# Attention steps 7 to 15 with scores ahead of the value product and row maxima ahead of its output's halves; four top-k instructions moved from steps 5 and 6 to step 3

## Chip, cores and metric

The kernel runs on one core of one Trainium2 chip. The metric is the device time of one execution in microseconds (us); lower is better.

## What is computed

One decoder block on 512 tokens of width 1024: a combined input projection, a gated mixer (A), a sparse attention (B), a gated merge, a feed-forward part and a final norm, all in float32. The change lies in mixer B. Cut to what matters:

```python
def block(i):                                   # 128 queries, i = 0..3
    score = sum_h wib[h] * relu(qib[h] @ ki.T)  # the indexer
    score = where(causal, score, -inf)
    sel_score, sel_idx = lax.top_k(score, 128)  # 128 keys of each query
    att = q @ k[sel_idx].T * 128 ** -0.5        # 8 heads, 2 key heads
    p = softmax(where(isfinite(sel_score), att, NEG_INF))
    return p @ v[sel_idx]
```

The kernel doesn't gather. It turns the scores of the indexer into a mask over all keys (0 for a chosen one, -1e30 else) by 16 rounds of "find the 8 largest, overwrite them", and adds the mask to the full scores before the softmax.

## The kernel before

The tile scheduler is switched off: every engine executes its instructions in the order in which the Python code issues them, and waits at an instruction until what it needs is there. So the order of the calls in the code is the order of each engine's queue.

A float32 product is made of three TensorE matmuls on rounded halves (`mm3`, L107 to L109: high by high, low by high, high by low). So every operand is first split: ScalarE (ACT in the profile) copies the high half, VectorE (DVE) subtracts it from the source to give the low half.

**Units and steps.** Attention runs over 16 units u, in `aun`: query block i = 3, 2, 1, 0 (512, 384, 256, 128 keys) by four pairs of heads. `at_step(s)` runs for s = 0 to 18, each step a slice of a pipeline over units. Steps and units are counted from 0 here. NT = 4: units 0 to 3 have their probabilities transposed by VectorE and a trip through DRAM, units 4 to 15 by TensorE. NU = 16. The pieces, with the letters used below:

- qk(u), `at_qk`: scores of unit u, six matmuls into PSUM banks 2 and 3 (two for the last four units).
- soft_a(u), `at_soft_a`: on VectorE, two instructions (L1394) that read qk(u) and the mask `sco`, and give masked scores and row maxima; then a scaling of the maxima (L1396). Until it has read them, banks 2 and 3 are taken.
- exp(u), `at_exp`, on ScalarE (L1404). inv(u), `at_inv`: reciprocal of the sums on VectorE (L1409) and one head's scaling on ScalarE (L1411); soft_b(u): the other head's scaling on VectorE (L1420). From unit 9 on soft_b does both, with the reciprocal (L1418).
- T(u), `at_T`: transposes on TensorE (pT, L1461), then th(u) on ScalarE (L1466) and tl(u) on VectorE (L1467), their high and low halves. For units 0 to 3: turn(u) on VectorE (tn, L1425), out(u) to DRAM by SyncE's queue (L1432), ld(u) back by GpSimd's queue (POOL, L1438), and halves th(u), tl(u) by `at_halves` (L1448, L1449).
- pv(u), `at_pv`: the value product, 3 matmuls for each 128 keys, into PSUM bank 0 (bank 1 for units 0 to 3). yb(u), `at_yb`: its output's halves, high on ScalarE (L1489), low on VectorE (L1490).
- `gb_part(n)`: matmuls of another projection, pgb, six for each of its 32 parts, that fill TensorE between the attention's pieces. `GBN` says how many parts each step takes: none in step 8, one in step 7, two in steps 9 to 15.

A step s from 7 on issues inv(s-1), pv(s-3), yb(s-3), qk(s), soft_a(s), T(s-2), soft_b(s-1), the split of a later query, exp(s), and then pgb; steps 5 to 8 also carry pv(s-5) and yb(s-5).

**Top-k** of blocks 2 and 1 isn't finished when attention starts. Its instructions lie in a list `bg` in order; `run_bg(us)` takes as many from it as the given budget pays by a cost written beside each. `need_sco(i)` in `at_soft_a` empties the list up to block i's mask if it isn't complete when it is needed. The dictionary in `at_step` sets the budget of each step.

Weights come by SyncE's queue into three buffers `raw`, and are split into `hi` (L164) and `lo` (L168), 128 by 1024 at a time; L263 is a weighted row sum on VectorE for later stages.

Of the kernel before, what the change touches and what calls it, by code (L numbers as in the profile page):

```python
# [58 lines left out]
def block_kernel(ctx: ExitStack, tc: tile.TileContext, x, x_t, w_in,  # L59
# [36 lines left out]
    def bank(k, name="bank"):  # L96
        return (two[0] if k > 5 else psum).tile([128, 512], F32, name=name, tag=f"b{k}", bufs=1)

    def f(ap):
        return ap.bitcast(F32)  # L100
# [4 lines left out]
    def mm3(o, wl, rl, start, stop, **kw):  # L105
        (wh, wlo), (rh, rlo) = wl, rl
        T.matmul(o, wh, rh, start=start, stop=False, **kw)  # L107
        T.matmul(o, wh, rlo, start=False, stop=False, **kw)  # L108
        T.matmul(o, wlo, rh, start=False, stop=stop, **kw)  # L109
# [357 lines left out]
    def t512(name, dt=F32):  # L467
        return base.tile([128, 512], dt, name=name, tag="t512", bufs=3)
# [444 lines left out]
    def run_bg(us):  # L913
        owed[0] += us
        while bg and owed[0] > 0:
            cost, fn = bg.popleft()
            fn()
            owed[0] -= cost

    def need_sco(i):  # L920
        while len(bg) > left.get(i, 99):
            bg.popleft()[1]()
# [402 lines left out]
    def at_split(u, apart=False):  # L1325
        i, hp = aun[u]
        if i == 0:
            return lambda: None
        qh = mid.tile([128, 2, 128], F32R, name="qh", tag="qh", bufs=2)
        ql = mid.tile([128, 2, 128], F32R, name="ql", tag="ql", bufs=2)  # L1330
        AS["q", u] = (qh, ql)
        src = qf[hp][:, :, i * 128:(i + 1) * 128]
        A.activation(qh, src, AF.Copy)
        if apart:
            return lambda: V.tensor_sub(ql, src, f(qh))
        V.tensor_sub(ql, src, f(qh))
# [25 lines left out]
    NU = len(aun)  # L1362
    gbp, gbt, gbn = {}, {}, [0]
    S2B, yb = [], []
    NT = 4
    pd = [dram.tile([32, 4096], F32, name=f"pd{k}") for k in range(NT)]

    def at_qk(u):
        i, hp = aun[u]
        nn = (i + 1) * 128  # L1370
        g = hp // 2
        for e in range(2):
            p = bank((4 if u < NT and u % 2 else 2) + e, "qk")
            AS["s", u, e] = p
            if i == 0:
                T.matmul(p[:, :nn], qf[hp][:, e, :nn], k_pl[:, g], start=True, stop=True)
                continue
            qh, ql = AS["q", u]
            mm3(p[:, :nn], (qh[:, e], ql[:, e]), (kk[0][:, g, :nn], kk[1][:, g, :nn]), True, True)

    def at_soft_a(u):
        i, hp = aun[u]
        need_sco(i)
        n = (i + 1) * 128
        k = u % 2 if u < NT else (u - NT + 2) % 3
        if k == 2:
            pt = [t512("pt"), t512("pt")]
        else:
            t = mid.tile([128, 2, S], F32, name="pt", tag=f"A{k}", bufs=1)
            pt = [t[:, 0], t[:, 1]]  # L1390
            AS["w", u] = t
        mx = tiny.tile([128, 8], F32, name="mx", tag="mx", bufs=3)
        for e in range(2):
            V.tensor_tensor_reduce(out=pt[e][:, :n], in0=AS["s", u, e][:, :n], in1=sco[i], scale=1.0,  # L1394
                                   scalar=-3.4e38, op0=OP.add, op1=OP.max, accum_out=mx[:, e:e + 1])
        V.tensor_scalar(mx[:, 2:4], mx[:, 0:2], -SCALE, None, op0=OP.mult)  # L1396
        AS["p", u] = (pt, mx)
# [9 lines left out]
    def at_inv(u):  # L1407
        pt, mx = AS["p", u]
        V.reciprocal(mx[:, 6:8], mx[:, 4:6])  # L1409
        n = (aun[u][0] + 1) * 128  # L1410
        A.mul(pt[1][:, :n], pt[1][:, :n], mx[:, 7:8])  # L1411

    def at_soft_b(u):
        i, hp = aun[u]
        n = (i + 1) * 128
        pt, mx = AS["p", u]
        if u >= NT + 5:
            V.reciprocal(mx[:, 6:8], mx[:, 4:6])  # L1418
        for e in range(1 if u < NT + 5 else 2):
            V.tensor_scalar(pt[e][:, :n], pt[e][:, :n], mx[:, 6 + e:7 + e], None, op0=OP.mult)  # L1420

    def at_turn(u):
        t = AS["t", u] = (mid if u < 3 else base).tile([128, 4, 4, 2, 32], F32, name="tn", tag=("G2", "G3", "G2", "gate")[u],
                                                       bufs=1)
        V.transpose(t.rearrange("p c k e j -> p e k c j"),  # L1425
                    AS["w", u].rearrange("p e (k c j) -> p e k c j", c=4, j=32))

    def at_out(u):
        t = AS["t", u].rearrange("p c k e j -> p (c k) (e j)")
        to = pd[u].rearrange("a (m r x) -> r a m x", r=4, x=64)  # L1430
        for r in range(4):
            SY.dma_start(to[r], t[32 * r:32 * r + 32])  # L1432

    def at_in(u):
        t = AS["l", u] = (mid if u % 2 else vmid).tile([128, 1024], F32, name="ld", tag="G1" if u % 2 else "L", bufs=1)
        rows = pd[u].rearrange("a (c m) -> c a m", c=4)
        for c in range(4):
            P.dma_start(t[32 * c:32 * c + 32], rows[c])  # L1438
# [12 lines left out]
    def at_T(u):  # L1451
        i, hp = aun[u]
        pt, _ = AS["p", u]
        th, tl = AS["t", u] = th_tl("A2", "A3")
        ev = []
        for s0 in range(0, i + 1, 2):
            ns = min(2, i + 1 - s0)
            p = bank(4 + s0 // 2, "pT")
            for s in range(ns):
                for e in range(2):  # L1460
                    T.transpose(p[:, (s * 2 + e) * 128:(s * 2 + e + 1) * 128],  # L1461
                                pt[e][:, (s0 + s) * 128:(s0 + s + 1) * 128], ident)
            o, ol = (x[:, s0:s0 + ns].rearrange("p s n -> p (s n)") for x in (th, tl))
            ev.append((o, ol, p[:, :ns * 256]))
        for o, ol, p in ev:
            A.activation(o, p, AF.Copy)  # L1466
            V.tensor_sub(ol, p, f(o))  # L1467

    def at_pv(u):
        i, hp = aun[u]  # L1470
        th, tl = AS["t", u]
        g = hp // 2
        p = bank(1 if u < NT else 0, "pv")
        for s in range(i + 1):
            mm3(p[:, :256], (v_hi[:, s, g * 128:(g + 1) * 128], v_lo[:, s, g * 128:(g + 1) * 128]),
                (th[:, s], tl[:, s]), s == 0, s == i)
        AS["o", u] = p[:, :256]

    def at_yb(u):
        i, hp = aun[u]  # L1480
        o = slice(i * 128, (i + 1) * 128)
        yh, yl = S2B[hp][:, :, o], S2B[4 + hp][:, :, o]
        p = AS["o", u]
        if u < NT:
            yh, yl = (x.rearrange("p e (r j) -> p e r j", r=4) for x in (yh, yl))
            p = p.rearrange("p (r e j) -> p e r j", r=4, e=2)
        else:
            p = p.rearrange("p (e n) -> p e n", e=2)
        A.activation(yh, p, AF.Copy)  # L1489
        V.tensor_sub(yl, p, f(yh))  # L1490
# [30 lines left out]
    def at_step(s):  # L1521
        if 1 <= s <= NT + 5:
            at_inv(s - 1)
        if s == 0:
            at_qk(0)
            at_split(2)
        pvs = [u for u in (s - 5, s - 3) if 0 <= u < NU and (u < NT) == (u == s - 5)]
        for u in pvs[-1:] if s >= NT + 3 else []:
            at_pv(u)
            at_yb(u)  # L1530
        q = s + 1 if s + 1 < NT else s if s >= NT else NU
        if q < NU:
            at_qk(q)
        if s < NU:
            at_soft_a(s)
        if s == 2:
            pa_last[0]()
        if NT <= s - 2 < NU:
            at_T(s - 2)
        if 0 < s <= NU:  # L1540
            at_soft_b(s - 1)
        if 2 <= s < NT + 2:
            at_in(s - 2)
        if 1 <= s < NT + 1:
            at_turn(s - 1)
            at_out(s - 1)
        n = s + 3 if s + 1 < NT else s + 2
        low = at_split(n, True) if n < NU and s != NT - 1 else lambda: None
        if s < NU:
            at_exp(s)  # L1550
        low()
        run_bg({0: 2.0, 1: 0.5, 5: 0.5, 6: 1.8, 7: 1.8}.get(s, 0))
        if s == NT:
            at_halves(0)
        if s - 5 in range(NT):
            gb_part(GBN[s] // 2)
            at_pv(s - 5)
            at_yb(s - 5)
        gb_part(GBN[s] - (GBN[s] // 2 if s - 5 in range(NT) else 0))
        if s - 4 in range(1, NT):  # L1560
            at_halves(s - 4)
        if s >= NT + 4:
            gb_evac()
# [3 lines left out]
    def pa_tasks():  # L1567
        au_tasks()
        at_step(pa_step[0])
        pa_step[0] += 1  # L1570
# [18 lines left out]
    for s in range(2, NU + 3):  # L1589
        at_step(s)  # L1590
# [500 lines left out]
    for q in range(-2, NQ):  # L2091
        g, u = 2 + q // 2, q % 2
# [299 lines left out]
```

## Time and profile before

| what | value |
|---|---|
| median of 3 runs (lowest, highest) | 783.99 us (782.96, 785.48) |
| the profiled execution's own time | 783.45 us |
| its span | 781.7 us |
| granted TensorE clock in it | 0.996 |
| busy share of the span: TensorE, VectorE, ScalarE, GpSimd | 98%, 87%, 60%, 24% |
| steps 2 to 18 of the attention in the span | about 290 to 369 us |
| TensorE's waits for other engines in the trace after 370 us | none shown |

In rows of the timeline the columns are start, duration, engine, line, operation, output and inputs, shape, how many were merged, and in brackets the idle time of the engine ahead of it with what released it. A window's row gives for each engine its busy time and how many instructions lie in it, then the granted clock (1.00 is full), the share of the DMA engines and GB/s. A TensorE matmul's end is modelled: how fast matmuls run is read from start to start. A row of the waits tells who waited for whom, the sum, how often and the longest.

### The profile page before, as it was taken

The page shows a single profiled execution, that of the slowest core. Times are in us where ns is not written, and L with a number is a line of the kernel's source. Part 1 is how long each engine was busy: PE and PEld are TensorE (multiplying, and loading weights), DVE is VectorE, ACT ScalarE, POOL GpSimd, SP SyncE. Part 2 cuts the span into 40 slices and gives each one's busy share as a digit, 9 for nine tenths or more (in the row PEclk, how much of TensorE's full clock was granted, in tenths as well). Part 3 has the DMA queues.
Part 4 walks back from the last instruction along what each step waited for, and adds up shares of the span by engine and source line. Part 5 has one row for each costly group of instructions (what it writes and reads, how often), then busy time and mean ns, then how long its engine had stood idle before and what let it go on. Part 6 is the DMA issues. An engine that isn't in the chain of part 4 may idle for free.

```text
span 781.7 us, 13086 instructions
## 1 busy us (share of the span) xinstructions
PE 767.6 (98%) x4867; PEld 695.9 (89%) x4867; DVE 677.0 (87%) x1108; ACT 469.4 (60%) x831; POOL 185.9 (24%) x270
## 2 busy tenths in 40 slices
PE   8999999999999999899999999999999999999996
PEld 6899899999888888788888899999999999888885
DVE  8879768888899998887797879989999888998886
ACT  6665568577443347666446677555666666666654
POOL 4882322320164503100010000322121322100002
PEclk9999999999999999999999999999999999999999
DMA  9957676986779739539592503979797967656762
GB/s 344 415 193 175 160 195 185 260 216 197 212 239 267 219 91 230 137 93 377 196 277 48 195 2 108 254 236 309 247 283 211 275 197 200 176 182 207 219 223 111
DMA packets 58978, 163.43 MB, mean 209 GB/s; under 512 B 17121, under 2 KB 17761, under 8 KB 58914
## 3 DMA queue, kind: packets, MB, share of 16 engines
q1 hardware_dynamic: 44240, 118.63, 44.7%
q0 software_dynamic: 14096, 43.01, 24.4%
q10 hardware_dynamic: 578, 0.95, 0.3%
q8 instruction: 38, 0.62, 0.3%
q14 instruction: 26, 0.21, 0.1%
HBM read 152.06 MB, written 33.30 MB: 237 GB/s over the span
## 4 chain that ended last, share of the span: by engine, by line
PE 84%; DVE 9%; DMA 2%; ACT 2%; issue 2%; POOL 1%; SPq 0%; POOLq 0%; DVEq 0%; ACTq 0%
PE R L107 8%; PE R L108 8%; PE R L109 8%; PE pb L109 5%; PE pb L108 5%; PE pb L107 5%; PE pfo L109 4%; PE pfo L108 4%; PE pfo L107 4%; PE pav L107 3%; PE pav L108 3%; PE pav L109 3%; PE po L109 2%; PE po L107 2%; PE po L108 2%; DVE sco L901 2%
## 5 line engine op out<-in xcount | busy, mean ns | idle before, releaser
L164 ACT ACTIVATE hi<-raw 128x1024 fp32r<-128x1024 f32 (+4 forms) x90 | 90.3, 1007 | 73.3 <-PE pfo L109 21.8
L168 DVE TENSOR_TENSOR lo<-raw,hi 128x1024 fp32r<-128x1024 f32 (+3 forms) x70 | 81.7, 1168 | 19.8 <-ACT hi L164 18.9
L108 PE MATMUL pfo<-lo,za 128*128 128x512 f32 (+1 forms) x144 | 55.2, 383 | 0.0
L109 PE MATMUL pfo<-hi,za 128*128 128x512 f32 (+1 forms) x144 | 55.2, 383 | 0.0
L107 PE MATMUL pfo<-hi,za 128*128 128x512 f32 (+1 forms) x144 | 55.2, 383 | 0.0
L107 PE MATMUL pb<-h,hi 128*128 128x512 f32 (+1 forms) x128 | 48.5, 379 | 0.0
L109 PE MATMUL pb<-h,lo 128*128 128x512 f32 (+1 forms) x128 | 48.1, 376 | 0.0
L108 PE MATMUL pb<-h,hi 128*128 128x512 f32 (+1 forms) x128 | 48.1, 376 | 0.0
L426 POOL COPY sm<-sm 128x1 f32<-128x1 f32 x36 | 25.6, 710 | 82.4 <-ACT sm L425 82.4
L108 PE MATMUL R<-tb,hi 128*128 128x256 f32 x160 | 44.2, 276 | 0.0
L107 PE MATMUL R<-tb,sx 128*128 128x256 f32 x160 | 44.2, 276 | 0.0
L108 PE MATMUL R<-tb,sx 128*128 128x256 f32 x160 | 44.2, 276 | 0.0
L109 PE MATMUL R<-tb,sx 128*128 128x256 f32 x160 | 44.2, 276 | 0.0
L107 PE MATMUL R<-tb,hi 128*128 128x256 f32 x160 | 44.2, 276 | 0.0
L109 PE MATMUL R<-tb,lo 128*128 128x256 f32 x160 | 44.2, 276 | 0.0
L168 POOL TENSOR_TENSOR lo<-raw,hi 128x1024 fp32r<-128x1024 f32 x12 | 30.6, 2548 | 31.0 <-ACT hi L164 31.0
L406 POOL DMA_DIRECT2D wsum<-in_w_ffn_out_dram x24 | 19.6, 838 | 73.3 <-DMA wsum<-wsum 42.9
L107 PEld LDWEIGHTS pfo<-hi,za 128*128 128x128 f32 x144 | 27.1, 188 | 5.4
L108 PEld LDWEIGHTS pfo<-lo,za 128*128 128x128 f32 x144 | 27.1, 188 | 5.3
L109 PEld LDWEIGHTS pfo<-hi,za 128*128 128x128 f32 x144 | 27.1, 188 | 5.2
L263 DVE CUSTOM_DVE_ANT_0 mraw<-mraw,csb,cols 128x1024 f32<-128x1024 f32 x20 | 28.4, 1426 | 2.0 <-DMA mraw<-in_w_shsc_dram 2.0
L108 PEld LDWEIGHTS R<-tb,hi 128*128 128x128 f32 x160 | 30.0, 188 | 0.0
(443 smaller groups left out, 2883.7 us busy)
## 6 DMA issues: line engine op xcount, KB each, us to landing
raw<-in_w_ffn_in_dram SPq DMA_DIRECT2D x44, 512.0 KB, 6.1
raw<-in_w_in_dram SPq DMA_DIRECT2D x36, 512.0 KB, 4.8
wsum<-in_w_ffn_out_dram POOLq DMA_DIRECT2D x30, 512.0 KB, 8.0
mraw<-in_w_shsc_dram SPq DMA_DIRECT2D x28, 512.0 KB, 4.7
raw<-wsum SPq DMA_DIRECT2D x20, 512.0 KB, 3.6
s<-in_w_shsc_dram SPq DMA_DIRECT2D x14, 512.0 KB, 8.0
raw<-in_w_ffn_out_dram SPq DMA_DIRECT2D x13, 512.0 KB, 4.5
wsum<-wsum POOLq DMA_DIRECT2D x10, 512.0 KB, 5.9
```

Of the source, the lines that this page charges most:

```text
L107: T.matmul(o, wh, rh, start=start, stop=False, **kw)
L108: T.matmul(o, wh, rlo, start=False, stop=False, **kw)
L109: T.matmul(o, wlo, rh, start=False, stop=stop, **kw)
L164: A.activation(hi[:, :m], e["raw"][:, :m], AF.Copy)
L168: e["lo"].tensor_sub(lo[:, :m], e["raw"][:, :m], f(hi[:, :m]))
L263: V.tensor_tensor_reduce(out=raw[:, c], in0=raw[:, c], in1=(csb if s > 1 else pc)[:, c], scale=scale, scalar=sums.pop(0), op0=OP.mult, op1 ...
L406: P.dma_start(wsum_at(n, c), src, max_dma_last_dim=4096, accum_op=OP.add)
L426: P.tensor_copy(t, t)
L901: V.match_replace(out=sco[i], in_to_replace=m8s[i], in_values=sco[i], imm_value=TAKEN)
```

## The change

From step 7 to step 15 qk(s) is issued first after inv, ahead of pv(s-3), and soft_a(s) ahead of yb(s-3). The budget of top-k gets an entry for step 3 and a smaller one for step 6.

```diff
     def at_step(s):
         if 1 <= s <= NT + 5:
             at_inv(s - 1)
+        late_q = NT + 3 <= s < NU
+        if late_q:
+            at_qk(s)
         if s == 0:
             at_qk(0)
             at_split(2)
         pvs = [u for u in (s - 5, s - 3) if 0 <= u < NU and (u < NT) == (u == s - 5)]
         for u in pvs[-1:] if s >= NT + 3 else []:
             at_pv(u)
-            at_yb(u)
+            if not late_q:
+                at_yb(u)
         q = s + 1 if s + 1 < NT else s if s >= NT else NU
-        if q < NU:
+        if q < NU and not late_q:
             at_qk(q)
         if s < NU:
             at_soft_a(s)
+        if late_q:
+            at_yb(pvs[-1])
...
-        run_bg({0: 2.0, 1: 0.5, 5: 0.5, 6: 1.8, 7: 1.8}.get(s, 0))
+        run_bg({0: 2.0, 1: 0.5, 3: 1.8, 5: 0.5, 6: 0.9, 7: 1.8}.get(s, 0))
```

VectorE's queue in step 3, as a piece of the difference; tn is turn(2), sco_633 the mask of block 1, and the lo and the reciprocal behind belong to a weight and to step 4:

```order
 L1425 STREAM_TRANSPOSE tn<-pt 128x2x4x4x32
+L898 MAX m_3245<-sco_633 128x8
+L901 MATCH_REPLACE sco_633<-m_3245,sco_633 128x256
+L898 MAX m_3248<-sco_633 128x8
+L901 MATCH_REPLACE sco_633<-m_3248,sco_633 128x256
 L168 TENSOR_TENSOR lo<-raw,hi 128x1024
 L1409 RECIPROCAL mx<-mx 128x2
```

Two rounds of top-k now stand between turn(2) and the weight's low half.

VectorE's queue at the end of step 6 and the start of step 7, before (ql is the low half of a query, yb_3153 belongs to unit 1, yb_3152 to unit 4, the tl of L1449 to unit 2, the reciprocal to unit 6, L1394 to unit 7):

```order
L1335 TENSOR_TENSOR ql<-qf_604,qh 128x256
L901 MATCH_REPLACE sco_633<-m_3377,sco_633 128x256
L898 MAX m_3455<-sco_633 128x8
L901 MATCH_REPLACE sco_633<-m_3455,sco_633 128x256
L904 TENSOR_SCALAR sco_633<-sco_633 128x256
L1490 TENSOR_TENSOR yb_3153<-pv,yb_3149 128x2x128
L1449 TENSOR_TENSOR tl<-ld,th 128x512 x2
L1409 RECIPROCAL mx<-mx 128x2
L1490 TENSOR_TENSOR yb_3152<-pv,yb_3148 128x2x128
L1394 ISA pt,mx<-qk,sco_634 128x384
L1394 ISA mx 128x1
```

And now:

```order
L1335 TENSOR_TENSOR ql<-qf_604,qh 128x256
L1490 TENSOR_TENSOR yb_3153<-pv,yb_3149 128x2x128
L1449 TENSOR_TENSOR tl<-ld,th 128x512 x2
L1409 RECIPROCAL mx<-mx 128x2
L1394 ISA pt,mx<-qk,sco_634 128x384
L1394 ISA mx 128x1
L1394 ISA pt,mx<-qk,sco_634 128x384
L1394 ISA mx 128x1
L1396 TENSOR_SCALAR mx<-mx 128x2
L1490 TENSOR_TENSOR yb_3152<-pv,yb_3148 128x2x128
```

The four top-k instructions of step 6 are gone (its closing one, L904, stands in step 5 in the place of a MAX), and yb(4) has moved from ahead of soft_a(7) to behind it.

TensorE's queue at the start of step 8, as a piece of the difference (qk is unit 8, pv unit 5):

```order
 L108 MATMUL pgb<-h_146,hi 128x512
 L109 MATMUL pgb<-h_144,lo 128x512
+L107 MATMUL qk<-k_hi,qh 128x256
+L108 MATMUL qk<-k_lo,qh 128x256
+L109 MATMUL qk<-k_hi,ql 128x256
+L107 MATMUL qk<-k_hi,qh 128x256
+L108 MATMUL qk<-k_lo,qh 128x256
+L109 MATMUL qk<-k_hi,ql 128x256
 L107 MATMUL pv<-th,v_hi 128x256
 L108 MATMUL pv<-tl,v_hi 128x256
```

The six score matmuls stood behind pv(5)'s nine before and stand ahead of them now; T(6) follows in both. ScalarE's, GpSimd's and SyncE's queues keep their order, and no instruction is added or dropped.

## The prediction

> **What bounds the kernel now.** I read the page first, then the engines' busy time by windows, the waits in the attention stretch, and the timelines of TensorE, VectorE and ScalarE there.
>
> ```profile
> span 781.7 us, 13086 instructions
> ...
> PE 767.6 (98%) x4867; PEld 695.9 (89%) x4867; DVE 677.0 (87%) x1108; ACT 469.4 (60%) x831; POOL 185.9 (24%) x270
> ```
>
> TensorE is the engine that sets the time: a microsecond of it is a microsecond of the span. The windows show where it has holes; its busy time is the number behind the first comma.
>
> ```profile
> 310.00:320.00 10.00, 9.33 (x56) 8.00 (x56) 8.13 (x25) 7.77 (x20) 4.11 (x9) 1.00 1.06 265
> 320.00:330.00 10.00, 8.92 (x63) 7.75 (x61) 7.71 (x23) 6.40 (x17) 0.11 (x1) 1.00 0.32 77
> 330.00:340.00 10.00, 8.56 (x56) 7.78 (x57) 8.82 (x27) 8.07 (x22) 0.00 (x0) 1.00 0.08 13
> 340.00:350.00 10.00, 9.72 (x58) 8.37 (x57) 9.08 (x28) 5.10 (x13) 0.57 (x1) 1.00 0.38 119
> ...
> 370.00:390.00 20.00, 20.00 (x90) 16.57 (x89) 14.73 (x19) 10.77 (x12) 1.34 (x3) 1.00 0.59 202
> ```
>
> The holes lie in 310 to 350 us, the attention's steps 6 to 11, at a full granted clock (1.00); the row from 370 has none. In the waits of that stretch two pairs stand out: ScalarE waits for VectorE's row sums, and VectorE in turn for ScalarE's copies.
>
> ```profile
> ACT pt L1411 <- DVE mx L1409: 12.3, 8, 2.9
> ...
> DVE yb L1490 <- ACT yb L1489: 8.2, 9, 1.5
> ```
>
> That is a ring: yb(s-3) on VectorE waits for ScalarE's half of it, and soft_a(s), queued behind yb, is what exp(s) on ScalarE needs. TensorE pays at pv, which needs the low halves tl made behind both:
>
> ```profile
> 308.75 0.28 PE L107 MATMUL pv<-th,v_hi 128*128 128x256 f32 x1
> ...
> 310.17 0.40 PE L107 MATMUL pgb<-h,hi 128*128 128x512 f32 x1
> ...
> 311.56 0.33 PE L107 MATMUL qk<-k_hi,qh 128*128 128x384 f32 x1
> ...
> 317.25 0.40 PE L107 MATMUL pgb<-h,hi 128*128 128x512 f32 x1
> ...
> 324.84 0.28 PE L107 MATMUL pv<-th,v_hi 128*128 128x256 f32 x1
> 325.94 0.40 PE L108 MATMUL pv<-tl,v_hi 128*128 128x256 f32 x1 [0.82 <-DVE tl L1467]
> ...
> 326.98 0.28 PE L107 MATMUL qk<-k_hi,qh 128*128 128x256 f32 x1
> ...
> 327.69 0.82 PE L1461 MATMUL pT<-ident,pt 128*128 128x128 f32 x6
> ...
> 331.80 0.39 PE L108 MATMUL pv<-tl,v_hi 128*128 128x256 f32 x1 [1.03 <-DVE tl L1467]
> ...
> 332.84 0.28 PE L107 MATMUL qk<-k_hi,qh 128*128 128x256 f32 x1
> ...
> 333.57 0.82 PE L1461 MATMUL pT<-ident,pt 128*128 128x128 f32 x6
> 334.14 0.48 PE L107 MATMUL pgb<-h,hi 128*128 128x512 f32 x1
> ...
> 342.47 0.39 PE L108 MATMUL pv<-tl,v_hi 128*128 128x256 f32 x1 [0.28 <-DVE tl L1467]
> ```
>
> From start to start these rows give undisturbed prices: twelve pv matmuls 308.75 to 310.17, 1.42 us (nine: 1.06); six pgb 310.17 to 311.56, 1.39; six qk 326.98 to 327.69, 0.71 at 256 keys (1.06 at 384, by width); six transposes 333.57 to 334.14, 0.57. Between qk(6) at 311.56 and T(7) at 333.57 TensorE has two qk of each width (3.54), T(4), T(5), T(6) (1.71), 18 pgb (4.17), pv(1), pv(2), pv(3) at twelve (4.26) and pv(4), pv(5), pv(6) at nine (3.18): 16.9 us of work in 22.0 us. So 5.1 us are lost there. The busy rows from 310 to 350 show only 3.5 us idle (40 less 36.53), since a matmul behind a wait is drawn longer. By the Trainium skill's "Perfetto Trace Analysis" (Identifying the Most-Contended Engine) matmul busy time is a bad measure because matmuls are pipelined; the trace agrees (5.1 by pace against 3.5 by idle). By the idle alone the gain forecast below would need nearly every hole closed, by the pace it leaves a third open.
>
> **The change, part by part.** The code of the changed order adds no instruction and drops none. The step that moves issues no transfer, and ScalarE's, GpSimd's and SyncE's queues keep their order; what changes is when their waits end. Once step 5 has run L904 the top-k list is empty, so the budgets of steps 6 and 7 buy nothing now.
>
> *Top-k into step 3.* VectorE's rows:
>
> ```profile
> 300.46 1.25 DVE L1425 STREAM_TRANSPOSE tn<-pt 128x1024 f32<-128x1024 f32 x1
> 302.52 1.23 DVE L168 TENSOR_TENSOR lo<-raw,hi 128x1024 fp32r<-128x1024 f32 x1 [0.82 <-ACT hi L164]
> ...
> 315.10 1.29 DVE L1449 TENSOR_TENSOR tl<-ld,th 128x512 fp32r<-128x512 f32 x2 [0.51 <-ACT th L1448]
> ...
> 319.30 0.08 DVE L901 MATCH_VALUE_LOAD sco<-m,sco 128x8 f32 x1
> ...
> 320.28 0.09 DVE L901 MATCH_VALUE_LOAD sco<-m,sco 128x8 f32 x1
> ...
> 321.34 1.28 DVE L1449 TENSOR_TENSOR tl<-ld,th 128x512 fp32r<-128x512 f32 x2
> ...
> 324.05 0.55 DVE L1394 CUSTOM_DVE_ANT_0 pt<-qk,sco 128x384 f32<-128x384 f32 x1
> ...
> 325.20 1.01 DVE L1467 TENSOR_TENSOR tl<-pT,th 128x512 fp32r<-128x512 f32 x2
> 326.13 0.41 DVE L1420 TENSOR_SCALAR pt<-pt,mx 128x384 f32<-128x384 f32 x1
> ```
>
> A round lasts 0.98 us (319.30 to 320.28), two 1.96. They start when turn(2) ends near 301.65, so the weight's lo moves from 302.52 to about 303.6: 0.82 us of idle time hides part, and VectorE runs some 1.06 us late through soft_a(4) and soft_a(5). TensorE has no hole before 313 and qk(5), qk(6) still find their banks free. ScalarE's exp(5), yb(0) and the next hi come 1.06 late too, but ahead of th(1) ScalarE had slack:
>
> ```profile
> 314.44 1.15 ACT L1448 ACTIVATE th<-ld 128x512 fp32r<-128x512 f32 x2 [1.10 <-DMA ld<-pd]
> ...
> 318.14 0.61 ACT L1404 ACTIVATE pt<-pt,mx 128x384 f32<-128x384 f32 x1
> ...
> 319.60 1.15 ACT L1448 ACTIVATE th<-ld 128x512 fp32r<-128x512 f32 x2
> ...
> 322.79 0.62 ACT L1411 ACTIVATE pt<-pt,mx 128x384 f32<-128x384 f32 x1 [2.04 <-DVE mx L1409]
> ...
> 323.58 0.86 ACT L1466 ACTIVATE th<-pT 128x512 fp32r<-128x512 f32 x2
> ...
> 325.32 0.61 ACT L1404 ACTIVATE pt<-pt,mx 128x384 f32<-128x384 f32 x1 [0.58 <-DVE mx L1396]
> ...
> 326.80 1.14 ACT L1448 ACTIVATE th<-ld 128x512 fp32r<-128x512 f32 x2
> ```
>
> So th(1) stays at 314.44. The lo that VectorE does ahead of tl(1) waits for its hi; it ended at 314.59 (315.10 less the 0.51 idle) and ends 1.06 later, near 315.6. So tl(1) moves from 315.10 to about 315.6. TensorE's pv(1) waits 0.48 us more. That is a loss; its ends are 0 (all hidden) and 1.45 (the full 1.96 less the 0.51). I take 0.48, since both waits in the way, 0.82 and 1.10, are in rows.
>
> *Top-k out of step 6.* exp(6) keeps the 0.48, so th(2) moves from 319.60 to 320.08. Its first half is there at 320.7, VectorE has no top-k in front, and tl(2) starts at 320.72 in place of 321.34, ending at 322.0: 0.6 us won, not 1.6, because ScalarE is next.
>
> *Scores and maxima first.* In the times of the changed kernel: pv(1) ends and pgb starts at 317.73 (was 317.25), six pgb to 319.12, qk(7) to 320.18, pv(4) to 321.24, T(5) to 321.81, pv(2) to 323.23 without a wait (its last low half came at 322.0), six pgb to 324.62. On VectorE soft_a(7) now follows the reciprocal at 322.0 in place of 324.05; it takes 1.15 with the maxima (324.05 to 325.20), to 323.15. ScalarE has inv(6) at 322.15, yb(4), th(5) at 322.95 (0.74, the next instruction is at 324.32), the query's split, exp(7) at 324.05 in place of 325.32, with its maxima long there. VectorE: yb(4) at 323.15, tl(5) 323.48 to 324.41 (0.93, 325.20 to 326.13). So in step 8 TensorE does qk(8) 324.62 to 325.33, pv(5) to 326.39 without the 0.82 us wait, T(6) to 326.96. ScalarE's th(3) comes at 325.53 in place of 326.80, tl(3) ends at 327.4, pv(3) runs 326.96 to 328.38, and qk(9) to 329.09, its banks freed by soft_a(8) at 328.2. ScalarE reaches th(6) at 328.43, and tl(6) has its first half at 329.6, so pv(6) waits about 0.5 and ends at 330.60. T(7) starts at 330.60 in place of 333.57: 2.97 us won, with 2.2 of the 5.1 us left (pv(1) 1.7, pv(6) 0.5).
>
> *Steps 10 to 18.* pgb fills two parts of each step to 14 and single ones later; the holes left by pace are small: the pv(8) row's wait and two like it, about 1.3 us together. The 0.71 us (0.45 in the last four units) of qk now pass ahead of pv and cover a part; soft_a no longer waits for yb's ScalarE half. I take 0.3, between 0 and 1.3.
>
> The banks: qk(s) at the head of a step waits for soft_a(s-1), but tl(s-3), which pv always needed, stands behind that soft_a in VectorE's queue, so this can't become a later wait than the old one. The new wait on VectorE is soft_a(s) for qk(s): behind it stand yb(s-3), tl(s-2) and a weight's lo; before, yb(s-3) waited in that place for pv(s-3) and ScalarE, which ended later.
>
> The sum is 3.0 + 0.3 = 3.3 us, already net of the 0.48: a span of 778.4 and, with the 1.75 us around it that the profiled execution had (783.45 less 781.7), 780.15. The median before is 0.54 above that execution, so 780.7. Behind 370 us TensorE waits for nothing; weights are loaded when earlier ones are used up, so that stretch should move forward as a whole.
>
> **The rivals.** *The probabilities of unit 3 come late.* turn(3) is a lagging piece of VectorE, and its way leads through DRAM:
>
> ```profile
> 318.04 2.08 POOL L1438 DMA_DIRECT2D ld<-pd  x4 [5.16 <-DVE mx L1396]
> ...
> DMA to landing us min/median/max: 2.9/5.1/6.9
> ```
>
> The last of the four ld(3) starts near 319.6 and, one lag later, near 320.7; it lands at 323.6 to 327.6. I have th(3) at 325.53, so at the long end TensorE loses up to 2.0 us at pv(3). The same step can lose to a smaller gain in the ring. Of the 3.3 us 1.0 to 2.3 stay: 781.7 to 783. For it speak the short slack and a busy DMA share of 1.06 in the row from 310; against it the share of 0.32 from 320, by when little else runs. [...]
>
> *The move of top-k costs and the order gains nothing.* If pv's waits in steps 7 to 9 hang on ScalarE's chain (exp, yb, th in its own order, which isn't changed), the new order moves idle time only. Then the 1.96 us in step 3 land in full on pv(1), with another 0.5 from the later ld(3): 786.5. It decides if ScalarE is the later one at th(5); against it stands its own 2.04 us idle ahead of inv(6), waiting for VectorE.
>
> *More is won.* If all holes up to step 11 but the one for ld(1) close, it is 4.5 us or more: below 779.5.
>
> *It doesn't do what it says.* The instructions stand in the new order on both engines, so I give this nothing.
>
> **How the numbers follow.** A measurement of this kernel can tell some 0.3%, 2.35 us: faster means below 781.6, slower above 786.3. My forecast, a gain of 2.4 to 4.5 us, gets 0.64; more than that 0.04; a smaller gain or none, mostly unit 3 late, 0.26; the slower case 0.06. The likeliest is 780.7. The range is 778.7 (780.7 less 1.0 for the later steps at their upper end, 0.5 for a pv(1) without the lag and 0.5 for a pv(6) without its wait) to 783.9 (nothing left of the gain).
>
> **What would show it.** In the changed profile soft_a(7) starts near 322.0, TensorE's wait in pv(5) is gone, T(7) starts near 330.6, pv(1)'s wait for tl is longer by 0.5, and the row from 370 has no hole. A wait of pv(3) for ld, or th(5) behind a busy ScalarE, would prove me wrong, and so would a TensorE hole after 345 us that wasn't there.

## The result, and the profile after

The changed kernel takes 779.99 us (median of 6 runs, 779.61 to 780.5) where the kernel before takes 783.79 (6 runs beside them, 782.96 to 785.48): a ratio of 0.995, 95% interval 0.9937 to 0.9963. That is 3.8 us by the medians; between the two profiled executions (783.45 and 779.98) it is 3.5, and 3.4 by span:

```profile
span 778.3 us, 13087 instructions
...
PE 766.5 (98%) x4867; PEld 696.3 (89%) x4867; DVE 677.7 (87%) x1108; ACT 468.4 (60%) x831; POOL 186.6 (24%) x270
```

The busy times are those of before within 1.1 us and the five instruction counts are the same: work was neither added nor dropped, so what went is idle time. The windows show where; TensorE's busy time stands behind the first comma.

```profile
310.00:320.00 10.00, 8.92 (x52) 7.58 (x52) 8.46 (x24) 7.39 (x19) 3.79 (x8) 1.00 0.98 241
320.00:330.00 10.00, 9.69 (x76) 9.14 (x76) 8.88 (x26) 8.04 (x22) 0.00 (x0) 1.00 0.28 91
330.00:340.00 10.00, 10.00 (x64) 9.03 (x64) 9.35 (x30) 7.34 (x22) 0.00 (x0) 1.00 0.29 79
340.00:350.00 10.00, 10.00 (x64) 8.91 (x64) 9.63 (x34) 6.30 (x18) 1.11 (x2) 1.00 0.50 171
...
370.00:390.00 20.00, 20.00 (x90) 16.56 (x89) 16.23 (x19) 8.90 (x11) 1.35 (x3) 1.00 0.57 208
```

The first row has become worse (8.92 for 9.33) and the three behind it are nearly full. TensorE's idle time over the four falls from 3.5 to 1.4 us. The timeline of TensorE names what is left:

```profile
312.73 0.82 PE L1461 MATMUL pT<-ident,pt 128*128 128x128 f32 x6
...
316.38 0.38 PE L108 MATMUL pv<-tl,v_hi 128*128 128x256 f32 x1 [0.95 <-DVE tl L1449]
...
321.19 0.82 PE L1461 MATMUL pT<-ident,pt 128*128 128x128 f32 x6
...
326.36 0.82 PE L1461 MATMUL pT<-ident,pt 128*128 128x128 f32 x6
...
328.98 0.28 PE L109 MATMUL qk<-k_hi,ql 128*128 128x256 f32 x1
...
329.84 0.39 PE L108 MATMUL pv<-tl,v_hi 128*128 128x256 f32 x1 [0.31 <-DVE tl L1467]
330.89 0.82 PE L1461 MATMUL pT<-ident,pt 128*128 128x128 f32 x6
...
365.23 0.40 PE L107 MATMUL pb<-yb,hi 128*128 128x512 f32 x1
```

The four pT rows are T(4), T(5), T(6) and T(7); the pb row is the first matmul behind the attention's last pv. Two waits are left, pv(1) for tl(1) (0.95 for the 0.34 of before) and pv(6) for tl(6) (0.31). qk(9), which stood behind pv(6), now ends ahead of it. T(7) starts 2.68 us earlier than before (333.57). In the trace of before the pb row stands here:

```profile
368.72 0.40 PE L107 MATMUL pb<-yb,hi 128*128 128x512 f32 x1
```

So 3.49 us are won by then, and from there to the end both kernels take 413 us (781.7 less 368.72, 778.3 less 365.23). VectorE after:

```profile
301.85 0.39 DVE L898 MAX8 m<-sco 128x8 f32<-128x256 f32 x1
...
303.66 1.21 DVE L168 TENSOR_TENSOR lo<-raw,hi 128x1024 fp32r<-128x1024 f32 x1
...
313.55 0.42 DVE L1490 TENSOR_TENSOR yb<-pv,yb 128x256 fp32r<-128x256 f32 x1 [0.79 <-ACT yb L1489]
314.50 1.23 DVE L168 TENSOR_TENSOR lo<-raw,hi 128x1024 fp32r<-128x1024 f32 x1 [0.53 <-ACT hi L164]
315.64 1.29 DVE L1449 TENSOR_TENSOR tl<-ld,th 128x512 fp32r<-128x512 f32 x2
...
320.27 0.43 DVE L1490 TENSOR_TENSOR yb<-pv,yb 128x256 fp32r<-128x256 f32 x1 [0.34 <-ACT yb L1489]
...
322.08 0.54 DVE L1394 CUSTOM_DVE_ANT_0 pt<-qk,sco 128x384 f32<-128x384 f32 x1
...
323.21 0.42 DVE L1490 TENSOR_TENSOR yb<-pv,yb 128x256 fp32r<-128x256 f32 x1
```

soft_a(7) starts at 322.08 for 324.05. yb(4) behind it, at 323.21, finds ScalarE's half there; in the trace of before it waited in front, as one of five idle places on VectorE between turn(2) and soft_a(7): 0.82 ahead of lo and 0.51 ahead of tl(1) (shown in the prediction), and these:

```profile
312.43 0.42 DVE L1490 TENSOR_TENSOR yb<-pv,yb 128x256 fp32r<-128x256 f32 x1 [0.65 <-ACT yb L1489]
313.37 1.22 DVE L168 TENSOR_TENSOR lo<-raw,hi 128x1024 fp32r<-128x1024 f32 x1 [0.52 <-DMA pd<-tn]
...
323.71 0.42 DVE L1490 TENSOR_TENSOR yb<-pv,yb 128x256 fp32r<-128x256 f32 x1 [1.01 <-ACT yb L1489]
```

Together 3.51 us before; 0.79, 0.53 and 0.34 make 1.66 after. The runs below are compared by this sum.

### The profile page after: what moved, and what is told of

Its sections match the earlier page's. It is cut to its first block, busy times and chain, and to the rows that moved or that the text cites. A ratio compares the mean times of both kernels' runs of the same rounds, so it can differ in the third digit from the quotient of the medians.

```text
span 778.3 us, 13087 instructions
## 1 busy us (share of the span) xinstructions
PE 766.5 (98%) x4867; PEld 696.3 (89%) x4867; DVE 677.7 (87%) x1108; ACT 468.4 (60%) x831; POOL 186.6 (24%) x270
## 4 chain that ended last, share of the span: by engine, by line
PE 86%; DVE 8%; DMA 2%; ACT 2%; issue 2%; POOL 0%; POOLq 0%; SPq 0%; DVEq 0%; ACTq 0%
PE R L108 8%; PE R L107 8%; PE R L109 8%; PE pb L107 5%; PE pb L108 5%; PE pb L109 5%; PE pfo L108 4%; PE pfo L109 4%; PE pfo L107 4%; PE pav L107 3%; PE pav L108 3%; PE pav L109 3%; PE po L109 2%; PE po L107 2%; PE po L108 2%; DVE sco L901 2%
## 5 line engine op out<-in xcount | busy, mean ns | idle before, releaser
L168 DVE TENSOR_TENSOR lo<-raw,hi 128x1024 fp32r<-128x1024 f32 (+3 forms) x70 | 81.8, 1170 | 19.6 <-ACT hi L164 19.3
L406 POOL DMA_DIRECT2D wsum<-in_w_ffn_out_dram x24 | 19.6, 839 | 79.8 <-DMA wsum<-wsum 45.7
L107 PEld LDWEIGHTS R<-tb,sx 128*128 128x128 f32 x160 | 30.1, 188 | 0.0
```

Source lines behind the costliest of these rows:

```text
L168: e["lo"].tensor_sub(lo[:, :m], e["raw"][:, :m], f(hi[:, :m]))
L406: P.dma_start(wsum_at(n, c), src, max_dma_last_dim=4096, accum_op=OP.add)
```

## The experiments

The theory ahead of them was the prediction's: yb's wait for ScalarE in front of soft_a is what costs, so VectorE's order brings most of the gain, TensorE's a smaller part, and the top-k move a little. The rivals put the gain elsewhere, or a loss on the top-k move; each expectation has its own. Twelve runs followed, in three series, each beside the kernel before (783.55, 783.63 and 783.77 us). Nothing is left out of the computation in any of them.

**New order, old top-k.** The budgets of before stay:

```diff
-        run_bg({0: 2.0, 1: 0.5, 3: 1.8, 5: 0.5, 6: 0.9, 7: 1.8}.get(s, 0))
+        run_bg({0: 2.0, 1: 0.5, 5: 0.5, 6: 1.8, 7: 1.8}.get(s, 0))
```

> The new order of scores and maxima in steps 7 to 15, with the top-k budgets of before. My theory (the order breaks the ring of yb and soft_a; top-k's move only adds 0.5 to 0.9 us): soft_a(7) starts near 322.6, pv(1) waits no longer than before, T(7) starts near 331.2, and the time is 2.4 to 2.9 us below before, 781.1. Rival (taking top-k out of step 6 is what frees VectorE): at most 1 us below before, 782.8 or more.

Measured: 779.62 us (779.29 to 780.46; ratio 0.9956, interval 0.9944 to 0.9969), so 3.9 below before, where 2.4 to 2.9 were expected. T(7) came at 330.91 where 331.2 was expected. The part of the theory that gave top-k 0.5 to 0.9 us falls: its move is worth nothing that can be measured. VectorE in steps 6 and 7:

```profile
320.29 0.29 DVE L904 TENSOR_SCALAR sco<-sco 128x256 f32<-128x256 f32 x1
320.50 0.42 DVE L1490 TENSOR_TENSOR yb<-pv,yb 128x256 fp32r<-128x256 f32 x1
320.84 1.28 DVE L1449 TENSOR_TENSOR tl<-ld,th 128x512 fp32r<-128x512 f32 x2
...
322.11 0.53 DVE L1394 CUSTOM_DVE_ANT_0 pt<-qk,sco 128x384 f32<-128x384 f32 x1
```

Top-k, which ends with the first of these rows, delays tl(2), but yb(1) then finds ScalarE's half there and doesn't idle, and soft_a(7) starts at 322.11, as in the changed kernel.

**Old order, new top-k.** All lines of the new order are undone:

```diff
-        late_q = NT + 3 <= s < NU
-        if late_q:
-            at_qk(s)
...
-            if not late_q:
-                at_yb(u)
+            at_yb(u)
...
-        if late_q:
-            at_yb(pvs[-1])
```

> The old order, with top-k moved to step 3. My theory: pv(1) waits 0.5 us more as in the changed kernel, the ring stays, soft_a(7) comes about 0.7 us earlier than before, and the time is 0.3 to 0.9 us below before, 783.2. Rival (top-k carries the gain): 2 us or more below before. The slower rival of the prediction (the lag lands in full): 1.5 to 2.5 us above before.

Measured: 783.21 us (11 runs, 782.27 to 784.96; ratio 0.9997, interval 0.9989 to 1.0006). The median is where the theory had it, but the interval contains no change at all. The wait ahead of yb(4) stays:

```profile
322.71 0.42 DVE L1490 TENSOR_TENSOR yb<-pv,yb 128x256 fp32r<-128x256 f32 x1 [1.01 <-ACT yb L1489]
323.06 0.55 DVE L1394 CUSTOM_DVE_ANT_0 pt<-qk,sco 128x384 f32<-128x384 f32 x1
```

The rival by which the top-k move costs 2 us or more is out.

**New order on TensorE alone.** yb goes back ahead of soft_a:

```diff
-            if not late_q:
-                at_yb(u)
+            at_yb(u)
...
-        if late_q:
-            at_yb(pvs[-1])
```

> As the changed kernel, but yb(s-3) stays ahead of soft_a(s) on VectorE: only TensorE's order is new. My theory (the wait of VectorE for ScalarE's half of yb is what delays soft_a): little more than top-k's part, 0.5 to 1.2 us below before, 783.0, with soft_a(7) near 323.3. Rival (it is TensorE's order that pays: qk done under pv's wait): 2.5 us or more below before, at most 781.3.

Measured: 782.63 us (11 runs, 782.03 to 783.56; ratio 0.9992, interval 0.9983 to 1.0), about 0.9 below before by the medians; the interval reaches from nothing to 1.3. The rival's 2.5 us or more are out. TensorE gets a wait that neither kernel had, qk(9) for the maxima of unit 8, which stand behind yb(5):

```profile
330.17 0.38 PE L107 MATMUL qk<-k_hi,qh 128*128 128x256 f32 x1 [0.92 <-DVE mx L1394]
```

**New order on VectorE alone.** qk goes back behind pv:

```diff
-        if late_q:
-            at_qk(s)
...
-        if q < NU and not late_q:
+        if q < NU:
             at_qk(q)
```

> As the changed kernel, but qk(s) stays behind pv(s-3) on TensorE: only VectorE's order is new. My theory: soft_a(7) near 322.0 all the same, pv(5) without a wait, but pv(6) waits over 1 us for tl(6) because qk(9) no longer stands ahead of it: 2.2 to 3.0 us below before, 781.2. Rival (TensorE's order pays): under 1.2 us below before, 782.6 or more.

Measured: 780.7 us (780.4 to 781.65; ratio 0.997, interval 0.9958 to 0.9982), 2.85 below before. VectorE's order carries most of the gain. TensorE waits in pv(6), since qk(9) isn't there to fill that time, but not over 1 us for tl(6) as expected: 0.44 for th(6) and then 0.30 for tl(6).

```profile
328.83 0.36 PE L107 MATMUL pv<-th,v_hi 128*128 128x256 f32 x1 [0.44 <-ACT th L1466]
```

**New order in steps 7 to 9 alone.** The second series asks where the gain arises.

```diff
-        late_q = NT + 3 <= s < NU
+        late_q = NT + 3 <= s < NT + 6
```

> The new order of TensorE and VectorE in steps 7, 8 and 9 alone; from step 10 on the order of before. Theory (the gain is the waits of pv(5), pv(6) and of the unit between, so nearly all of it arises before T(7)): T(7) near 330.9 us, and T(9) and the first matmul behind the attention only 2.7 to 3.1 us earlier than before, so 780.5 to 780.9 where before has 783.6; the 0.3 to 0.7 us that are missing against the full change are what steps 10 to 18 add. Rival (each step of the nine gives an equal part): a third of 3.6 us, 782.4. Second rival (the old order in step 10 brings the ring back as soon as VectorE and ScalarE meet it, and takes the gain away): a wait of one of the later pv of 0.5 us or more that neither before nor the changed kernel has, 781.5 or above.

Measured: 780.67 us (780.37 to 781.56; ratio 0.9964, interval 0.9952 to 0.9977), the time that the theory had. T(7) comes at 330.16, in an execution that ran 0.7 us ahead of the changed kernel's already in step 3 (turn(2) ended at 301.14 for 301.85). Behind T(7) one wait grows, pv(8)'s for tl(8), from 0.28 us before to 0.56:

```profile
339.39 0.39 PE L108 MATMUL pv<-tl,v_hi 128*128 128x256 f32 x1 [0.56 <-DVE tl L1467]
...
365.62 0.40 PE L107 MATMUL pb<-yb,hi 128*128 128x512 f32 x1
```

From T(7) to pb this takes 35.46 us, before 35.15, the changed kernel 34.34. So the new order in steps 10 to 15 is worth 1.1 us against this kernel and 0.8 against before, by the traces; by the medians this kernel and the changed one differ by 0.7. The second rival's sign, a later pv that waits 0.5 us or more, did come; its price, 781.5 or above, did not.

**One top-k round in step 3, one in step 5.** Step 5 has idle places of 0.79 and 0.53 us on VectorE in the changed kernel.

```diff
-        run_bg({0: 2.0, 1: 0.5, 3: 1.8, 5: 0.5, 6: 0.9, 7: 1.8}.get(s, 0))
+        run_bg({0: 2.0, 1: 0.5, 3: 0.9, 5: 1.4, 6: 0.9, 7: 1.8}.get(s, 0))
```

> The changed kernel with one of the two top-k rounds left in step 3 and the other put into step 5, ahead of L904, where VectorE has idle time of 0.8 and 0.5 us. Theory (the lag of VectorE in step 3 is what makes pv(1) wait 0.5 us longer, and the early top-k is what spares tl(2) 0.6 us): the lag falls to about 0.2 us, pv(1)'s wait for tl goes from 0.95 back to about 0.4 us, tl(2) keeps its gain, and the time is 0.4 to 0.5 us below the changed kernel: about 779.3 where before has 783.6. Rival (tl(1) is set by the landing of ld(1), and what is saved at pv(1) is lost at tl(2), as in the run with the new order alone): no difference from the changed kernel or from the order alone, 779.6 to 779.9.

Measured: 778.97 us (778.53 to 779.24; ratio 0.994, interval 0.9927 to 0.9953), 1.0 below the changed kernel: the direction was right, the size twice the 0.4 to 0.5 expected. VectorE:

```profile
312.44 0.42 DVE L1490 TENSOR_TENSOR yb<-pv,yb 128x256 fp32r<-128x256 f32 x1
313.31 1.22 DVE L168 TENSOR_TENSOR lo<-raw,hi 128x1024 fp32r<-128x1024 f32 x1 [0.45 <-ACT hi L164]
...
319.08 0.42 DVE L1490 TENSOR_TENSOR yb<-pv,yb 128x256 fp32r<-128x256 f32 x1 [0.35 <-ACT yb L1489]
...
320.89 0.54 DVE L1394 CUSTOM_DVE_ANT_0 pt<-qk,sco 128x384 f32<-128x384 f32 x1
```

Only 0.80 us of idle time is left between turn(2) and soft_a(7). I had counted the 0.5 us at pv(1) and not that everything on VectorE up to soft_a(7) moves with it.

**All of step 6's pgb ahead of pv(1).** This gives TensorE work in its largest remaining hole:

```diff
-            gb_part(GBN[s] // 2)
+            gb_part(GBN[s] if s == 6 else GBN[s] // 2)
...
-        gb_part(GBN[s] - (GBN[s] // 2 if s - 5 in range(NT) else 0))
+        gb_part(GBN[s] - (GBN[s] if s == 6 else GBN[s] // 2 if s - 5 in range(NT) else 0))
```

> The changed kernel with all twelve pgb matmuls of step 6 ahead of pv(1) instead of half of them, so that TensorE has work while tl(1) is being made; nothing is left out. Theory (behind pv(1) the chain over tl(4), tl(2) and tl(6) on VectorE and ScalarE, and not TensorE, sets the time up to pv(6)): pv(1)'s wait for tl of 0.95 us disappears, but what TensorE gains there it loses again at pv(2) and pv(6), whose waits grow: 0 to 0.4 us below the changed kernel, 779.4 to 779.9 where before has 783.6. Rival (a TensorE hole is worth its full length, 1.7 us by pace, wherever it lies): T(7) near 329.5 us and 778.2 to 778.7.

Measured: 779.58 us (779.28 to 780.14; ratio 0.995, interval 0.9936 to 0.9963). The wait of pv(1) is gone and a wait of pv(2) takes its place; T(7) is at 330.74, and not near 329.5:

```profile
321.38 0.39 PE L108 MATMUL pv<-tl,v_hi 128*128 128x256 f32 x1 [0.34 <-DVE tl L1449]
...
330.74 0.82 PE L1461 MATMUL pT<-ident,pt 128*128 128x128 f32 x6
```

TensorE's hole was not worth its length: T(7) keeps its distance from turn(2) (29.04 us here and in the changed kernel), for VectorE was the later one further on.

**Both of these edits.**

> The two last edits together: one top-k round in step 3 and one in step 5, and all pgb of step 6 ahead of pv(1). Theory (the second half of the hole is closed by the filler, and tl(1), tl(2) come early): pv(1) and pv(2) don't wait, pv(6) waits 0.3 to 0.8 us for tl(6), 0.5 to 0.9 us below the changed kernel, 778.9 to 779.3 where before has 783.6. Rival (ScalarE's chain over th(2), th(5), th(3), th(6) sets T(7) whatever TensorE does ahead): equal to the changed kernel within 0.3 us, 779.5 to 780.0.

Measured: 779.32 us (778.64 to 780.07; ratio 0.9944, interval 0.993 to 0.9958). That lies at the upper end of what the theory had, 778.9 to 779.3, and below the rival. T(7) comes at 329.65 and without the filler edit at 329.68: the gain is that of the top-k placement, and the filler adds nothing to it. The 0.35 us between the two medians are not seen in the traces (pb at 363.96 here, 364.01 without the filler).

**Three more MAX8 in step 5.** The third series adds cost where it is suspected: work on VectorE that nothing uses, in an idle place here and one step later in the next run.

```diff
         run_bg({0: 2.0, 1: 0.5, 3: 1.8, 5: 0.5, 6: 0.9, 7: 1.8}.get(s, 0))
+        for _ in range(3 if s == 5 else 0):
+            V.max(tiny.tile([128, 8], F32, name="mx8", tag="mx8", bufs=1), sco[1])
```

> The changed kernel with three more MAX8 on VectorE (each about 0.46 us from start to start, 1.38 together; their results are used by nothing), placed in step 5 behind L904, where VectorE idles 0.79 us ahead of yb(0) and 0.53 us ahead of lo. Theory (from step 3 to soft_a(7) VectorE's own row of work, with its idle places, sets the time, so only work that misses an idle place costs): yb(0) near 314.1 in place of 313.55, lo still at 314.50, soft_a(7) still near 322.1, T(7) near 330.9, and the time as the changed kernel's, 779.8 to 780.2. Rival (every added microsecond of VectorE in this stretch costs its length): 1.4 us more, 781.3.

Measured: 780.49 us (780.16 to 780.6; ratio 0.9954, interval 0.9942 to 0.9967).

```profile
312.73 1.35 DVE L1560 MAX8 mx<-sco 128x8 f32<-128x256 f32 x3
314.00 0.41 DVE L1490 TENSOR_TENSOR yb<-pv,yb 128x256 fp32r<-128x256 f32 x1
314.44 1.23 DVE L168 TENSOR_TENSOR lo<-raw,hi 128x1024 fp32r<-128x1024 f32 x1
...
322.02 0.54 DVE L1394 CUSTOM_DVE_ANT_0 pt<-qk,sco 128x384 f32<-128x384 f32 x1
```

The 1.27 us of MAX8 (312.73 to 314.00) fill the idle places ahead of yb(0) and lo (1.32 together), and soft_a(7) stays. By the trace the added work is free. The median is 0.5 to 0.6 above the changed kernel's two, more than the theory had and well under the rival's 1.4. Where that lies stays open: the profiled execution was the fastest of the five (780.16), and from turn(2) to pb it takes as long as the changed kernel.

**The same in step 6.** The edit is the same with `s == 6`.

> The same three MAX8 one step later, in step 6 ahead of yb(1), where VectorE idles 0.34 us only. Theory (VectorE's row sets the time): soft_a(7) 1.0 us later, 323.1, T(7) near 331.9, and 0.8 to 1.1 us above the changed kernel, about 781.0. Rival (ScalarE's chain or TensorE sets the time there, and VectorE has slack): within 0.3 us of the changed kernel.

Measured: 781.0 us (780.78 to 781.69; ratio 0.9963, interval 0.9951 to 0.9976), 1.1 above the changed kernel run beside it.

```profile
315.84 1.29 DVE L1449 TENSOR_TENSOR tl<-ld,th 128x512 fp32r<-128x512 f32 x2 [0.30 <-ACT th L1448]
...
320.04 1.34 DVE L1560 MAX8 mx<-sco 128x8 f32<-128x256 f32 x3
...
322.90 0.54 DVE L1394 CUSTOM_DVE_ANT_0 pt<-qk,sco 128x384 f32<-128x384 f32 x1
```

soft_a(7) is 1.0 us later. Of that 0.3 is the idle time ahead of tl(1), since the probabilities of unit 1 landed later in this execution; the MAX8 account for some 0.7. Whether that landing was late in the other four executions too, and so makes up the rest of the 1.1, no trace shows. That VectorE has slack there is out.

**The changed kernel again**, unaltered:

> The changed kernel once more, unaltered, as the measure for the others of this series: 779.7 to 780.3 where before has 783.6; in its trace soft_a(7) near 322.1 and T(7) near 330.9, so that 0.3 us between executions is what the readings of single traces are uncertain by.

Measured: 779.88 us (779.3 to 780.28; ratio 0.9947, interval 0.9935 to 0.996); soft_a(7) at 321.86, T(7) at 330.65.

**Old order, top-k in steps 3 and 5.** The edits of the second and the sixth kernel together:

> The order of before with the top-k rounds in steps 3 and 5. Theory (in the old order yb(4) waits for ScalarE's half of it, and what VectorE is ahead is lost there, so the round placed in idle time gains nothing): the wait of about 1.0 us ahead of yb(4) is there or longer, T(7) near 332.5, and 0.2 to 0.6 us below before as with the two rounds in step 3: 783.0 to 783.4. Rival (VectorE's row counts in any order): 1.0 us below the run with the two rounds in step 3, 782.2.

Measured: 782.15 us (11 runs, 781.75 to 784.6; ratio 0.9986, interval 0.9977 to 0.9996), 1.6 below before by the medians; the interval, 0.3 to 1.8, doesn't decide against the theory's 0.2 to 0.6, but the trace does. T(7) is at 332.08 and not near 332.5, and soft_a(7) comes 20.77 us after turn(2), where it took 21.68 with both rounds in step 3. My theory fell and the rival's number came:

```profile
322.26 0.42 DVE L1490 TENSOR_TENSOR yb<-pv,yb 128x256 fp32r<-128x256 f32 x1 [1.01 <-ACT yb L1489]
322.60 0.55 DVE L1394 CUSTOM_DVE_ANT_0 pt<-qk,sco 128x384 f32<-128x384 f32 x1
```

The wait ahead of yb(4) is there, but it doesn't swallow what VectorE is ahead: ScalarE's copy follows inv(6), which waits for VectorE's reciprocal, so ScalarE comes earlier by as much (inv(6) starts 0.25 to 0.26 us after the reciprocal in all four kernels with yb in front). At this place the ring is a price of 1.01 us, the same in each of the four, and no fixed point in time.

**The account of all runs.** Each column is read from the timelines: the idle time on VectorE between turn(2) and soft_a(7) (the sum of its rows' brackets), and three stretches: from turn(2)'s end to soft_a(7), from there to T(7), from T(7) to pb. turn(2)'s end is where the next instruction starts, 1.17 us after turn(2) itself; where VectorE idles then (the first two rows) the same 1.17 us are taken.

| kernel | idle | to soft_a(7) | to T(7) | to pb | median us |
|---|---|---|---|---|---|
| before | 3.51 | 22.42 | 9.52 | 35.15 | 783.8 |
| old top-k, new order | 1.99 | 20.56 | 8.80 | 34.38 | 779.62 |
| new top-k, old order | 2.67 | 21.68 | 9.48 | 35.15 | 783.21 |
| TensorE's order alone | 2.69 | 21.67 | 8.77 | 35.79 | 782.63 |
| VectorE's order alone | 1.67 | 20.23 | 9.53 | 34.55 | 780.7 |
| steps 7 to 9 alone | 1.66 | 20.23 | 8.79 | 35.46 | 780.67 |
| changed | 1.66 | 20.23 | 8.81 | 34.34 | 779.99 |
| changed again | 1.67 | 20.24 | 8.79 | 34.35 | 779.88 |
| top-k in 3 and 5 | 0.80 | 19.36 | 8.79 | 34.33 | 778.97 |
| pgb first | 1.66 | 20.22 | 8.82 | 34.32 | 779.58 |
| both | 0.78 | 19.32 | 8.83 | 34.31 | 779.32 |
| MAX8 in step 5 | 0.36 | 20.24 | 8.82 | 34.34 | 780.49 |
| MAX8 in step 6 | 1.61 | 21.24 | 8.80 | 34.35 | 781.0 |
| top-k in 3 and 5, old order | 1.78 | 20.77 | 9.48 | 35.19 | 782.15 |

The second column less the first is 18.5 to 18.6 us in every kernel with soft_a in front and without added work; with yb(4) in front it is 18.9 to 19.0, yb(4)'s own 0.34 us (323.71 to 324.05 in before) and a little more. The two with MAX8 have 19.9 and 19.6, the added work. A constant difference by itself says no more than that VectorE does the same work in each kernel. That VectorE's queue sets the time in this stretch is shown by the runs that add or move work: MAX8 where VectorE has little idle time make soft_a(7) later, the same MAX8 in an idle place don't, a round moved into an idle place brings soft_a(7) 0.9 us earlier in either order (20.23 to 19.36, 21.68 to 20.77), and more work for TensorE ahead of pv(1) changes nothing (20.22). ScalarE has a share in it, since most of VectorE's idle places end with a copy of ScalarE's; no run changed ScalarE's work alone.

The three stretches of a kernel, set against those of before, give its gain by the medians to within 0.6 us (the worst is the second row, 3.4 by the trace and 3.9 by the medians). Smaller differences between two medians are not explained by this table.

The third column has two values: 8.8 with qk ahead of pv, 9.5 with qk behind it. The difference of 0.7 is the six matmuls of qk(9) (0.71 us), which pass into pv(6)'s wait.

## Why the prediction came out right, step by step

**The bound.** TensorE's holes in 310 to 350 us were the place: nothing moved behind pb, and no hole opened after 345 us. By pace, from qk(6) to T(7), 2.3 of the 5.1 lost us are left (19.21 us for 16.86 of work), about the 2.2 of the prediction's sum; its remark that a third would stay open doesn't fit that sum. The forecast of 780.7 us was 0.7 above the measured 779.99: 0.17 of it lies in the forecast of a profiled execution (780.15 for 779.98), and 0.54 were added because the median before lay above its profiled execution, which it doesn't in the changed kernel.

By the Trainium skill's "Perfetto Trace Analysis" (Identifying the Most-Contended Engine) matmul busy time is not a good measure of how close a kernel is to its limit, because pipelined matmuls look smaller in the trace. These runs agree that it misleads, but here in the other direction, since a matmul behind a wait is drawn longer (0.39 us in the pv row at 329.84, 0.28 undisturbed): from qk(6) to pb, with the same matmuls, TensorE's idle time fell by 2.1 us (3.48 to 1.39) and the path by 3.6 (57.16 to 53.55).

**Top-k into step 3.** Foreseen: lo at 303.6, tl(1) at 315.6, 0.48 us more at pv(1). Measured: 303.66, 315.64, and 0.53 more (316.38 for 315.85; 0.41 counted from T(4)). The two covers that the sum named, 0.82 and 1.10 us, were used up as it said.

**Top-k out of step 6.** Foreseen: tl(2) at 320.72, 0.6 us won. Measured 320.79. The prediction booked the loss and the gain in two places and had their sum near zero; the runs with and without the move (779.62 and 779.99) give no difference. What it didn't see is why: the move fills the 0.82 us ahead of lo, but ScalarE becomes late by the same lag, and VectorE then idles 0.79 for 0.65 ahead of yb(0) and another 0.34 ahead of yb(1). The sums of idle time, 1.99 and 1.66, lie close, and the 0.3 us between them don't show in the medians.

**Scores and maxima first.** Foreseen: soft_a(7) at 322.0, no wait in pv(5), th(3) at 325.53, pv(6) with a wait of 0.5, T(7) at 330.60, 2.97 us earlier. Measured: 322.08, none, 325.55, 0.31, and 330.89; with 0.12 us that this execution was behind already at T(4) (312.73 for 312.61), 2.80 us. ScalarE's rows:

```profile
314.37 1.14 ACT L1448 ACTIVATE th<-ld 128x512 fp32r<-128x512 f32 x2
...
322.26 0.62 ACT L1411 ACTIVATE pt<-pt,mx 128x384 f32<-128x384 f32 x1 [0.98 <-DVE mx L1409]
...
324.09 0.62 ACT L1404 ACTIVATE pt<-pt,mx 128x384 f32<-128x384 f32 x1
...
325.55 1.16 ACT L1448 ACTIVATE th<-ld 128x512 fp32r<-128x512 f32 x2
```

The 2.68 us of T(7) are 1.97 of VectorE (soft_a(7)) and 0.71 of TensorE (qk(9) in pv(6)'s wait), and the two runs with one half each show both (20.23 us to soft_a(7) with VectorE's order alone, 8.77 from there to T(7) with TensorE's). In the 1.97 is what the top-k move does to soft_a(7): without it the new order alone brings soft_a(7) 1.86 us closer to turn(2), in the old order the move alone 0.74, both together 2.19.

**Steps 10 to 18.** This term was mis-sized: 0.3 us were taken, from between 0 and 1.3, and 0.8 were measured (35.15 less 34.34). Of the two causes that the prediction named, the runs with one half each tell which it is. With VectorE's order alone this stretch takes 34.55 us, 0.6 of the 0.8; with TensorE's alone it takes 35.79, longer than before. So most of it comes from soft_a no longer waiting behind yb, and qk ahead of pv adds 0.2 only together with that.

The two errors of the sum offset each other in part: up to T(7) 2.97 us were forecast and 2.68 came (2.80 from T(4)), behind it 0.3 and 0.8. That the span came out at 778.3 for the forecast 778.4 is to that extent luck; the mechanism and the place are not.

**The rivals.** Unit 3 was not late: GpSimd issued ld(3) at 317.97 (318.04 before), and th(3) had no wait.

```profile
317.97 1.93 POOL L1438 DMA_DIRECT2D ld<-pd  x4 [5.39 <-DVE mx L1394]
```

By the profile the idle time ahead of it ended on VectorE, and not with the landing of out(3). In the code ld(3) goes into the buffer of ld(1) (`at_in`) and has to wait for tl(1), which started at 315.64 here and at 315.10 before. So turn(3)'s lag of 1.1 us (306.58 for 305.46) was not the last wait, as the rival had taken it to be. By the Trainium skill's "SBUF — State Buffer" (Who interferes with whom) VectorE in a two-port mode and GpSimd exclude each other from a pair of ports that both use, which can starve GpSimd's writing of DMA descriptors. The four issues took 1.93 us, 2.08 before, so no such stretching is seen here. The rival in which top-k costs and the order gains nothing had ScalarE's chain as the later one: ScalarE still waits 0.98 us for VectorE ahead of inv(6), and top-k alone cost nothing. More than 4.5 us was not won by this change; with the top-k rounds in steps 3 and 5 it is 4.7 by the medians.

## What to carry to other kernels

Where an in-order engine paces a stage (added work there makes the stage longer), add up its idle places from one fixed instruction to the one that the stage waits for; an edit is worth the idle time that it takes out of that sum, and a lag that another engine hands back puts it in again. An instruction that waits for another engine belongs behind those that don't, and filler work on the engine that waits in the end gained nothing here while the pacing engine was unchanged. Moving background work out of the way only helps if it lands in an idle place that stays: here, against the old placement, two rounds in one place gained nothing that can be told, and one round each in two places gained 0.7 us in the new order and 1.6 us in the old one.

## What the runs showed of the hardware that was not expected

Two executions of one kernel can differ in when a stage begins and still agree inside the stage: turn(2) ended at 301.85 and at 301.62 in two profiled executions of the changed kernel, and from there soft_a(7) took 20.23 and 20.24 us, T(7) from there 8.81 and 8.79. So times are better taken from an instruction ahead of the edit in the same trace.

What GpSimd issues moved more: in the same two executions ld(3) started at 317.97 and at 316.99. In the run with MAX8 in step 6 th(1) waited for ld(1) until 315.18 where the changed kernel has 314.37, though nothing ahead of it in the queues was altered; the last piece of ld(1) was issued at 313.10 there and at 312.08 in the changed kernel. Why, these traces don't show.

```profile
315.18 1.15 ACT L1448 ACTIVATE th<-ld 128x512 fp32r<-128x512 f32 x2 [0.90 <-DMA ld<-pd]
```
